# Projections with the weights moving: 512 or 416 columns a bank in place of 256

## The chip, the cores and the metric

The kernel runs on one core of a Trainium2 chip. The metric is the device time of one execution in microseconds (us). A core has a matrix engine (TensorE, PE in the rows), a vector engine (VectorE, DVE), a scalar engine (ScalarE, ACT), a general engine (GpSimd, POOL) and an engine that issues the transfers here (SyncE, SP). They run side by side and wait for each other through semaphores.

## The reference, cut to what matters

Two layers over x of 512 tokens and 1024 features, and a memory of 256 tokens. The first layer mixes with A (attention over all tokens) and B (a window with a sink), the second with C (attention through low-rank latents) and D (a neighbourhood of the token grid). Each layer goes on with a cross-attention into the memory and a gated feed-forward part. The projections that the change touches are these:

```python
def mixer_ab(h, w_in, g_qa, g_ka, sink, w_out, ang_1d, ang_2d):
    qa, ka, va, qb, kb, vb = _split(h @ w_in, AB_SIZES)        # 512, 128, 128, 512, 128, 128
    qa = apply_rope(rms_norm(qa.reshape(B, S, A_HEADS, HEAD_DIM), g_qa), ang_2d)
    ...
    qb = apply_rope(qb.reshape(B, S, B_HEADS, HEAD_DIM), ang_1d)
    ...

def mixer_cd(h, w_in, g_cq, g_ckv, w_uq, w_ukv, rpb, w_out, ang_c):
    cq, ckv, kr, qd, kd, vd = _split(h @ w_in, CD_SIZES)       # 256, 128, 32, 512, 512, 512
    q = (rms_norm(cq, g_cq) @ w_uq).reshape(B, S, C_HEADS, C_NOPE + C_ROPE)
    ...

def memory_cross_attention(h, m, w_q, w_kv, w_o):
    k, v = jnp.split(m @ w_kv, 2, axis=-1)                     # 512, 512
    ...
```

## The kernel before, in words

Every product is made in three matmuls. `split` (L111) takes a matrix apart into a rounded high part and the low part that is left; `mm3` (L126 to 129) adds high x high (L127), high x low (L128) and low x high (L129) into one bank. The high part of weights is a cast on ACT (L117), or on POOL (L119) where an engine is named; the low part a subtraction (L123) on DVE, for some weights on POOL. x is held transposed, with features on the partitions: `xh` and `xl` are eight tiles each, one for every 128 features.

Weights come through three rings of buffers: `load` (L98) brings 1 MB or less by one transfer of SP's queue into one of two `raw` buffers, `split` writes its parts into one of four `wh` and one of four `wl` buffers of 1024 columns. A raw buffer is free once both parts are made, a `wh` and `wl` once the last matmul has read them. A bank holds 512 columns; there are two banks `mm`, two `S`, two `T`, one `X` and one `O`.

In the projections of this change x stays in the array and the weights move through it, so the tokens come out on the partitions. `natural` (L194) does this for 256 columns of weights: a bank takes two token tiles of 128 beside each other, 24 matmuls each, and then `evac` reads the bank. `natural_weights` (L190) makes two parts of four k-rows (blocks of 128 features) for it.

Mixers A and B (`mixer_ab`, L369): `kv_part` makes keys and values, `q_part` (L461) the queries of four heads in one call, so that each mixer calls it twice. Its `evac` scales and rotates the heads of one token tile (`rotate`, L411, with ACT at L415, `headnorm` for A, `rope_mul` at L364 to 367 on POOL and DVE), writes high and low halves (L471, L472), and transposes them on PE (L429). Then 32 units of attention, each one head and half of the tokens, go through `pipeline` with lags: scores (L492, L493) into S, softmax (`softmax_rows`, L239), transposes of the weights into T (L272), a high and a low part of them (L275, L276), product with the values (L550).

Mixer C (`mixer_cd`, L555): the latents are two calls of `natural`, at column 256 for the keys' and values' latents with the shared rotary key (L619, 160 of its 256 columns are used) and at column 0 for the queries' (L620). `lat_norm` (L590) normalizes on ACT (L594, L595) and DVE (L598). On the way the row sums of x squared are brought over the partitions: eight matmuls (L150), a power on DVE and POOL (L133, L134), four scalings of the identity on DVE (L183), and one matmul that spreads them (L185). `latT` transposes the latents (L625). `up_pair` (L635) makes keys, values and queries of two heads from them: 256 columns of `w_ukv`, and of `w_uq` 256 columns of which 192 are used, for it is called four times. `v_d` (L565) makes the values of mixer D by `natural` into banks T.

`memory_kv` (L817) makes the memory's keys and values for the cross-attention, the values by two loads of 256 columns with the low parts turn by turn on DVE and POOL.

No order of the engines' work is written by hand: the program is written once, and a planner that simulates time puts each engine's instructions in an order when the kernel is built. Each engine then runs its own list strictly in that order.

## Time and profile before

| what | us |
|---|---|
| median of 3 runs | 1412.44 (1411.24 to 1412.59) |
| profiled execution | 1410.33 |
| its span in the trace | 1408.3 |
| PE busy | 1374.1, 98% |
| DVE busy | 796.6, 57% |
| ACT busy | 632.8, 45% |
| POOL busy | 413.1, 29% |
| mean granted clock of PE | 0.997 |

The span is the time from the first to the last instruction of the core; the execution is 2.0 us longer. A busy engine is one with an instruction open; for PE the rows of consecutive matmuls overlap, so a matmul costs the distance from its start to the next one's. A granted clock of 1.00 is the full 2.4 GHz, 0.50 the lower level of 1.2 GHz. In a row's end, `[2.82 <-DVE ptl L276]` says that the engine stood still for 2.82 us before it and that a DVE instruction of line 276 on the tile ptl released it. `mm<-wh,xgh` reads: into mm, from wh (moving) and xgh (in the array).

### The profile page before, as it was taken

How to read it: one execution, taken by the hardware profiler on the slowest of the kernel's cores; microseconds unless marked ns; L12 is line 12 of the kernel's file. 1: busy time of each engine (PE TensorE's matmuls, PEld its weight loads, DVE VectorE, ACT ScalarE, POOL GpSimd, SP SyncE). 2: the span in 40 equal slices, each digit the busy share in tenths (PEclk: the TensorE clock that was granted, in tenths of full speed). 3: DMA queues.
4: the chain of work that ended last, by engine and by line, in shares of the span. 5: the costliest groups of instructions: out<-in, count | busy, mean ns of one | idle time of the engine just before them, and what ended most of it. 6: DMA issues, size and time to landing. Idle time of an engine off the chain costs nothing.

```text
span 1408.3 us, 20396 instructions
## 1 busy us (share of the span) xinstructions
PE 1374.1 (98%) x7835; PEld 1194.8 (85%) x7835; DVE 796.6 (57%) x1426; ACT 632.8 (45%) x1217; POOL 413.1 (29%) x503
## 2 busy tenths in 40 slices
PE   8898999999999999999999999999999999999997
PEld 8897889998888888888988888798988888888887
DVE  6988886763344334436578744657643353335355
ACT  5567785643221323323468554656533222222243
POOL 4855444212210121111324345752122111111121
PEclk9999999999999999999999999999999999999999
DMA  7110024321332223203221132324302322232111
GB/s 235 61 61 30 23 70 132 122 106 60 100 110 90 90 94 114 85 23 105 51 76 46 31 101 66 113 97 149 121 30 92 114 93 90 90 106 104 45 45 61
DMA packets 77514, 120.88 MB, mean 86 GB/s; under 512 B 5791, under 2 KB 64106, under 8 KB 71786
## 3 DMA queue, kind: packets, MB, share of 16 engines
q1 hardware_dynamic: 77418, 119.58, 26.3%
q8 instruction: 62, 1.02, 0.3%
q14 instruction: 34, 0.28, 0.1%
HBM read 117.47 MB, written 2.10 MB: 85 GB/s over the span
## 4 chain that ended last, share of the span: by engine, by line
PE 87%; DVE 8%; ACT 2%; issue 1%; DMA 1%; POOL 0%; SPq 0%; POOLq 0%; ACTq 0%; DVEq 0%
PE mm L127 12%; PE mm L128 12%; PE mm L129 12%; PE S L127 7%; PE S L128 7%; PE S L129 7%; PE T L128 6%; PE T L129 6%; PE T L127 6%; PE O L550 3%; PE T L272 2%; DVE wl L123 1%; PE X L129 1%; PE O L129 1%; PE X L127 1%
## 5 line engine op out<-in xcount | busy, mean ns | idle before, releaser
L117 ACT CAST wh<-rawgu 128x1024 fp32r<-128x1024 f32 x88 | 92.3, 1053 | 296.4 <-PE S L128 116.4
L117 ACT CAST wh<-raw 128x1024 fp32r<-128x1024 f32 (+2 forms) x116 | 115.0, 992 | 198.8 <-PE mm L128 53.4
L1029 POOL TENSOR_TENSOR act<-P,act 128x512 fp32r<-128x512 f32 x44 | 74.2, 1688 | 401.0 <-ACT act L1028 401.0
L127 PE MATMUL T<-xgh,wh 128*128 128x512 f32 x352 | 137.8, 391 | 0.0
L123 DVE TENSOR_TENSOR wl<-raw,wh 128x1024 fp32r<-128x1024 f32 (+2 forms) x98 | 123.3, 1260 | 24.8 <-ACT wh L117 23.5
L128 PE MATMUL S<-xgl,wh 128*128 128x512 f32 x352 | 137.2, 390 | 0.0
L127 PE MATMUL S<-xgh,wh 128*128 128x512 f32 x352 | 136.9, 390 | 0.1
L129 PE MATMUL S<-xgh,wl 128*128 128x512 f32 x352 | 137.0, 389 | 0.0
L129 PE MATMUL T<-xgh,wl 128*128 128x512 f32 x352 | 137.0, 389 | 0.0
L128 PE MATMUL T<-xgl,wh 128*128 128x512 f32 x352 | 136.9, 389 | 0.0
L123 DVE TENSOR_TENSOR wl<-rawgu,wh 128x1024 fp32r<-128x1024 f32 x88 | 116.4, 1325 | 28.5 <-ACT wh L117 27.9
L1025 DVE TENSOR_TENSOR P<-P,T 128x512 f32<-128x512 f32 x44 | 30.1, 688 | 138.5 <-PE T L129 137.1
L253 POOL TENSOR_SCALAR P<-P,sm 128x512 f32<-128x512 f32 (+2 forms) x128 | 81.5, 650 | 83.2 <-DVE sm L251 48.3
L1022 DVE TENSOR_TENSOR g<-S,bc 128x512 f32<-128x512 f32 x44 | 30.2, 691 | 130.5 <-PE S L129 124.9
L128 PE MATMUL mm<-act,wh 128*128 128x512 f32 (+1 forms) x264 | 99.0, 375 | 0.0
L127 PE MATMUL mm<-act,wh 128*128 128x512 f32 (+1 forms) x264 | 98.9, 375 | 0.0
L129 PE MATMUL mm<-act,wl 128*128 128x512 f32 (+1 forms) x264 | 98.8, 375 | 0.0
L276 DVE TENSOR_TENSOR ptl<-T,pth 128x512 fp32r<-128x512 f32 (+2 forms) x128 | 72.4, 583 | 21.1 <-ACT pth L275 20.7
L127 PEld LDWEIGHTS S<-xgh,wh 128*128 128x128 f32 x352 | 66.1, 188 | 14.7 <-DVE g L1022 0.9
L127 PEld LDWEIGHTS T<-xgh,wh 128*128 128x128 f32 x352 | 66.1, 188 | 14.2 <-issue 0.5
L128 PEld LDWEIGHTS T<-xgl,wh 128*128 128x128 f32 x352 | 66.1, 188 | 14.1 <-issue 0.5
L129 PEld LDWEIGHTS S<-xgh,wl 128*128 128x128 f32 x352 | 66.1, 188 | 13.7
(366 smaller groups left out, 3811.9 us busy)
## 6 DMA issues: line engine op xcount, KB each, us to landing
rawgu<-in_w_gate_up_dram SPq DMA_DIRECT2D x44, 1024.0 KB, 5.0
raw<-in_w_down_dram SPq DMA_DIRECT2D x16, 1024.0 KB, 5.2
raw<-in_w_xkv_dram SPq DMA_DIRECT2D x8, 1024.0 KB, 5.2
raw<-in_w_down_dram SPq DMA_DIRECT2D x8, 768.0 KB, 4.7
raw<-in_w_in_ab_dram SPq DMA_DIRECT2D x5, 1024.0 KB, 5.5
raw<-in_w_out_ab_dram SPq DMA_DIRECT2D x4, 1024.0 KB, 5.1
raw<-in_w_xq_dram SPq DMA_DIRECT2D x4, 1024.0 KB, 5.3
raw<-in_w_xo_dram SPq DMA_DIRECT2D x4, 1024.0 KB, 5.2
```

The lines of the kernel that those rows point to most:

```text
L117: nc.scalar.copy(hv, v)
L123: low.tensor_sub(lv[:, q], v[:, q], hv[:, q].bitcast(F32))
L127: nc.tensor.matmul(o, lh, rh, start=start, stop=False)
L128: nc.tensor.matmul(o, lh, rl, start=False, stop=False)
L129: nc.tensor.matmul(o, ll, rh, start=False, stop=stop)
L253: nc.gpsimd.tensor_scalar(p, p, ri[:, j:j + 1], 1.0, op0=ALU.mult, op1=ALU.mult)
L272: nc.tensor.transpose(tb_[:, i * P:(i + 1) * P], p[:, i * P:(i + 1) * P], ident)
L276: nc.vector.tensor_sub(ptl[:, k0:k1, j * P:(j + 1) * P], tv, hv.bitcast(F32))
L550: nc.tensor.matmul(ob[:, q0 + a:q0 + b], v_of(kt), pt[:, kt, a:b], start=(i == 0 and j == 0), stop=(i == n - 1 and j == 1), skip_group_che ...
L1022: nc.vector.tensor_mul(g, bg, bc)
L1025: nc.vector.tensor_mul(sg, sg, bu)
L1029: nc.gpsimd.tensor_sub(l, sg, h.bitcast(F32))
```

## The change

Two functions are new. `wide_weights` loads eight k-rows of n columns in two transfers of four k-rows and splits each in two, so that one projection's weights stand in four pairs of buffers of two k-rows. `wide` puts one token tile into a bank, n columns wide, and calls `evac` for every tile.

- The queries of A and of B are one projection of 512 columns each. The rotation runs over eight heads at a time; the high parts of all of A's query weights are made on POOL, before only those of the first call.
- The latents of C are one projection of 416 columns (queries' 0 to 255, keys' and values' 256 to 383, rotary key 384 to 415) in place of two of 256.
- `w_uq` is taken by 192 columns a pair, not 256.
- The memory's values are one projection of 512 columns; all their low parts are made on DVE.

```diff
+    def wide_weights(w, c0, n, eng=None):
+        parts = []
+        for i in range(2):
+            v = load(w[4 * i * P:4 * (i + 1) * P, c0:c0 + n].rearrange("(k p) n -> p k n", p=P), 4, n)
+            parts += [split(v[:, 2 * j:2 * j + 2], 2, n, eng) for j in range(2)]
+        return parts
+
+    def wide(xh, xl, parts, n, evac, nt=NT):
+        for tt in range(nt):
+            bank = mm_bank()[:, :n]
+            ts_ = slice(tt * P, (tt + 1) * P)
+            for k in range(KF):
+                wh, wl = parts[k // 2]
+                mm3(bank, xh[k][:, ts_], xl[k][:, ts_], wh[:, k % 2], wl[:, k % 2], k == 0, k == KF - 1)
+            evac(tt, bank)
...
-            def rotate(src3, scale, cs, tt, nh, norm):
-                rt = ph.tile([P, 3, 256], F32, tag="rt", bufs=4, name="rt")
+            def rotate(rt, src3, scale, cs, tt, nh, norm):
...
+            def rt_tile():
+                return ph.tile([P, 3, S], F32, tag="rt", bufs=2, name="rt")
...
             def q_part(isA, c0):
-                Q = [ph.tile([P, 2, S], F32R, tag="Q", bufs=4, name="Q") for _ in range(2)]
-                def evac(b, bank):
-                    n = ph.tile([P, 2, 4, P], F32R, tag="nst", bufs=2, name="nst")
-                    for j in range(2):
-                        tt = 2 * b + j
-                        qs = bank[j].rearrange("p (h d) -> p h d", h=4)
-                        r = rotate(qs, (rstd if isA else rstd8)[:, tt:tt + 1],
-                                   tabs["q"] if isA else tabs["B"], tt, 4, isA)
-                        alternate("qs").tensor_copy(n[:, j, :, 0:64], r)
-                        nc.vector.tensor_sub(n[:, j, :, 64:128], r, n[:, j, :, 0:64].bitcast(F32))
-                    to_stacks(n, Q, b)
-                natural(xh, xl, w_in, c0, evac, natural_weights(w_in, c0, nc.gpsimd) if isA and c0 == 0 else None)
+                Q = [ph.tile([P, 4, S], F32R, tag="Q", bufs=2, name="Q") for _ in range(2)]
+                def evac(tt, bank):
+                    n = ph.tile([P, 8, P], F32R, tag="nst", bufs=2, name="nst")
+                    r = rotate(rt_tile(), bank.rearrange("p (h d) -> p h d", h=8), (rstd if isA else rstd8)[:, tt:tt + 1],
+                               tabs["q"] if isA else tabs["B"], tt, 8, isA)
+                    alternate("qs").tensor_copy(n[:, :, 0:64], r)
+                    nc.vector.tensor_sub(n[:, :, 64:128], r, n[:, :, 0:64].bitcast(F32))
+                    for i in range(2):
+                        t = x_bank()
+                        for a in range(4):
+                            nc.tensor.transpose(t[:, a * P:(a + 1) * P].bitcast(F32R), n[:, 4 * i + a], identr)
+                        nc.scalar.copy(Q[i][:, :, tt * P:(tt + 1) * P], t.rearrange("p (a n) -> p a n", a=4))
+                wide(xh, xl, wide_weights(w_in, c0, S, nc.gpsimd if isA else None), S, evac)
                 return Q
...
-                    sa["Q"] += q_part(True, 0) + q_part(True, 256)
+                    sa["Q"] += q_part(True, 0)
...
-                    sb_["Q"] += q_part(False, 768) + q_part(False, 1024)
+                    sb_["Q"] += q_part(False, 768)
...
-            natural(xh, xl, w_in, 256, ckv_evac)
-            natural(xh, xl, w_in, 0, cq_evac)
+            def evac(tt, bank):
+                lat_norm(bank[:, 256:384], ckn[:, tt], tt, 128)
+                rw = ph.tile([P, 3, 32], F32, tag="rw", bufs=2, name="rw")
+                nc.scalar.activation(rw[:, 0], bank[:, 384:416], AF.Copy, scale=rstd[:, tt:tt + 1])
+                rope32(krn[:, tt:tt + 1], rw[:, 0:1], rw[:, 1:2], rw[:, 2:3],
+                       tcs[0][:, tt:tt + 1], tcs[1][:, tt:tt + 1])
+                lat_norm(bank[:, 0:256], cqn[tt // 2][:, tt % 2], tt, 256)
+            wide(xh, xl, wide_weights(w_in, 0, 416), 416, evac)
...
-                c0 = min(pr * 192, 512)
-                off = pr * 192 - c0
-                v = load(w_uq[0][:, c0:c0 + 256].rearrange("(k p) n -> p k n", p=P), 2, 256)
-                wh, wl = split(v, 2, 256)
+                v = load(w_uq[0][:, pr * 192:(pr + 1) * 192].rearrange("(k p) n -> p k n", p=P), 2, 192)
+                wh, wl = split(v, 2, 192)
...
-        for c in range(2):
-            v = load(wkv[:, 512 + c * 256:512 + (c + 1) * 256].rearrange("(k p) n -> p k n", p=P), KF, 256)
-            pr = [split(v[:, 4 * i:4 * i + 4], 4, 256, None, alternate("kv")) for i in range(2)]
...
+        def v_evac(t, bank):
+            parts(bank.rearrange("p (h d) -> p h d", h=2), vm)
+        wide(mh, ml, wide_weights(wkv, 512, S), S, v_evac, 2)
...
-                    mm3(ob, vm[0][c][:, k, vs], vm[1][c][:, k, vs], pth[:, k], ptl[:, k], k == 0, k == 1)
+                    mm3(ob, vm[0][k][:, c, vs], vm[1][k][:, c, vs], pth[:, k], ptl[:, k], k == 0, k == 1)
```

Lines behind the new functions have higher numbers in the changed kernel: L594 is L617 there, L595 is L618, L615 is L632, L625 is L642. In all PE issues 6851 rows of order where it issued 7233.

Two places of the engines' orders. The first is PE's list at the start of mixer C, around the row sums of the normalization. Before (34 matmuls of the same three kinds stand between L150 and L185):

```order
L128 MATMUL mm<-wl,xgh 128x256
L129 MATMUL mm<-wh,xgl 128x256
L150 MATMUL X<-ones,P 128x1 x4
L127 MATMUL mm<-wh,xgh 128x256
...
L129 MATMUL mm<-wh,xgl 128x256
L185 MATMUL X<-P,ones 128x512
```

and with the change:

```order
L129 MATMUL mm<-wh,xgl 128x416
L127 MATMUL mm<-wh,xgh 128x416
L150 MATMUL X<-ones,P 128x1 x4
L128 MATMUL mm<-wl,xgh 128x416
L129 MATMUL mm<-wh,xgl 128x416
L185 MATMUL X<-P,ones 128x512
L127 MATMUL mm<-wh,xgh 128x416
```

L185 stands two matmuls behind the sums, where it stood 34 behind them. 46 matmuls of the latents stand ahead of L150 in the change, and 48 behind L185.

The second is ACT's list over the latents, with the first cast of weights behind them: the up-projection's, 256 columns of `w_ukv`, then those of `w_uq`, then v_d's of 1024. Before:

```order
L594 ACTIVATE P<-mm,sm 128x128
L615 ACTIVATE rw<-mm,sm 128x32
L595 ACTIVATE P,sm<-P 128x128
L117 CAST wh<-raw 128x256
L595 ACTIVATE P,sm<-P 128x128
L594 ACTIVATE P<-mm,sm 128x128
```

and with the change:

```order
L617 ACTIVATE P<-mm,sm 128x128
L632 ACTIVATE rw<-mm,sm 128x32
L618 ACTIVATE P,sm<-P 128x128
L617 ACTIVATE P<-mm,sm 128x256
L117 CAST wh<-raw 128x256
L618 ACTIVATE P,sm<-P 128x256
L117 CAST wh<-raw 128x384
```

Before, the cast stood behind the first two token tiles of the first latents; now it stands behind the third of four tiles of the joined projection.

## Rows read from the trace of the kernel before

**Rows 1.** The page: busy time of TensorE, and shares of the chain.

```profile
PE 1374.1 (98%) x7835; PEld 1194.8 (85%) x7835; DVE 796.6 (57%) x1426; ACT 632.8 (45%) x1217; POOL 413.1 (29%) x503
...
PE 87%; DVE 8%; ACT 2%; issue 1%; DMA 1%; POOL 0%; SPq 0%; POOLq 0%; ACTq 0%; DVEq 0%
```

**Rows 2.** Windows: us, busy (x) of PE, PEld, DVE, ACT, POOL; clock; DMA; GB/s.

```profile
24.00:61.00 37.00, 35.17 (x295) 34.76 (x295) 35.72 (x92) 15.71 (x31) 31.32 (x41) 1.00 0.41 127
61.00:125.00 64.00, 60.11 (x463) 55.42 (x461) 57.30 (x117) 46.02 (x107) 38.71 (x55) 1.00 0.10 34
...
676.00:702.00 26.00, 25.13 (x202) 24.21 (x201) 11.96 (x39) 10.49 (x31) 9.24 (x15) 1.00 0.25 63
...
960.00:1010.00 50.00, 49.52 (x382) 47.66 (x382) 34.86 (x68) 30.15 (x69) 13.18 (x20) 1.00 0.39 131
```

**Rows 3.** Timeline of PE, 695.7 to 696.6: start, length, line, operation, shape.

```profile
695.76 0.28 PE L129 MATMUL mm<-wh,xgl 128*128 128x256 f32 x1
...
696.60 0.28 PE L127 MATMUL mm<-wh,xgh 128*128 128x256 f32 x1
```

**Rows 4.** Timeline of PE, 600.0 to 601.2.

```profile
600.06 0.39 PE L127 MATMUL S<-xgh,wh 128*128 128x512 f32 x1
...
601.19 0.39 PE L129 MATMUL S<-xgh,wl 128*128 128x512 f32 x1
```

**Rows 5.** Timeline of PE, 158.3 to 159.1.

```profile
158.49 0.28 PE L550 MATMUL O<-ptl,vst 128*128 128x128 f32 x1
158.60 0.67 PE L127 MATMUL mm<-o,wh 128*128 128x512 f32 x2
```

**Rows 6.** Groups by form, DVE, 20 to 170: busy us, mean ns, idle before.

```profile
L276 DVE TENSOR_TENSOR ptl<-T,pth 128x512 fp32r<-128x512 f32 x32 | 21.5, 683 | 3.4 <-ACT pth L275 3.2
...
L276 DVE TENSOR_TENSOR ptl<-T,pth 128x256 fp32r<-128x256 f32 x3 | 1.3, 417 | 0.0
```

**Rows 7.** Timeline of all engines, 122.6 to 129.

```profile
124.89 0.40 PE L493 MATMUL S<-K,Q 128*128 128x512 f32 x1
...
127.28 0.68 DVE L276 TENSOR_TENSOR ptl<-T,pth 128x512 fp32r<-128x512 f32 x1
...
128.11 0.63 PE L272 MATMUL T<-identr,P 128*128 128x128 f32 x4 [2.82 <-DVE ptl L276]
```

**Rows 8.** Windows of 2 us behind that place, columns as in rows 2.

```profile
130.00:132.00 2.00, 1.97 (x9) 1.70 (x9) 1.94 (x4) 1.78 (x6) 0.51 (x2) 0.50 0.80 274
132.00:134.00 2.00, 2.00 (x14) 1.96 (x13) 2.00 (x5) 1.37 (x3) 1.46 (x2) 0.67 0.00 0
```

**Rows 9.** Timeline, 676.2 to 690.3: the first latents and the row sums.

```profile
676.22 0.28 PE L127 MATMUL mm<-wh,xgh 128*128 128x256 f32 x1
...
687.31 0.37 ACT L594 ACTIVATE P<-mm,sm 128x128 f32<-128x128 f32 x1 [5.32 <-POOL sm L134]
687.31 0.87 DVE L183 TENSOR_SCALAR P<-identr,sm 128x128 f32<-128x128 f32 x4 [1.13 <-POOL sm L134]
...
690.00 0.59 PE L185 MATMUL X<-P,ones 128*128 128x512 f32 x1
```

**Rows 10.** Timeline, 688.5 to 702.7: the weights behind the latents.

```profile
688.76 0.41 ACT L117 CAST wh<-raw 128x256 fp32r<-128x256 f32 x1 [0.17 <-PE mm L129]
...
689.20 0.42 DVE L123 TENSOR_TENSOR wl<-raw,wh 128x256 fp32r<-128x256 f32 x1 [0.17 <-ACT wh L117]
...
689.65 0.37 SPq L101 DMA_DIRECT2D raw<-in_w_in_cd_dram  x1
...
701.12 1.05 ACT L117 CAST wh<-raw 128x1024 fp32r<-128x1024 f32 x1 [2.69 <-PE mm L129]
...
702.20 1.23 DVE L123 TENSOR_TENSOR wl<-raw,wh 128x1024 fp32r<-128x1024 f32 x1 [2.46 <-ACT wh L117]
...
702.36 0.60 PE L625 MATMUL X<-identr,P 128*128 128x128 f32 x4
```

**Rows 11.** DMA issues, 685 to 705: KB each, median us to landing.

```profile
raw<-in_w_in_cd_dram SPq DMA_DIRECT2D x1, 1024.0 KB, 5.8
```

More of the change, by code (lines that the diff above doesn't have):

```diff
@@ L439, in evac @@
                     n = ph.tile([P, 2, 4, P], F32R, tag="nst", bufs=2, name="nst")
+                    rt = rt_tile()
                     for j in range(2):
@@ L442, in evac @@
                         ks = bank[j][:, 0:128].rearrange("p (h d) -> p h d", h=2)
-                        r = rotate(ks, rstd[:, tt:tt + 1], tabs["k"] if isA else tabs["B"], tt, 2, isA)
+                        r = rotate(rt[:, :, j * 256:(j + 1) * 256], ks, rstd[:, tt:tt + 1], tabs["k"] if isA else tabs["B"], tt, 2, isA)
                         rb = r.unsqueeze(2).broadcast_to([P, 2, 2, 64])
@@ L483, in front @@
                         st["pre"](h)
-                    Q, K = st["Q"][h // 2], st["K"][kv]
+                    Q, K = st["Q"][h // 4], st["K"][kv]
                     tiles, offs = [], []
@@ L490, in front @@
                         sb = s_bank()[:, :n]
-                        qv = Q[:, h % 2, qt * P:(qt + 1) * P]
+                        qv = Q[:, h % 4, qt * P:(qt + 1) * P]
                         nc.tensor.matmul(sb, qv, K[:, 0, k0 * P:k1 * P], start=True, stop=False)
@@ L604, in rope32 @@
                 nc.vector.tensor_add(dst, t1, t2)
-            def cq_evac(b, bank):
-                for j in range(2):
-                    lat_norm(bank[j], cqn[b][:, j], 2 * b + j, 256)
-            def ckv_evac(b, bank):
-                for j in range(2):
-                    tt = 2 * b + j
-                    lat_norm(bank[j][:, 0:128], ckn[:, tt], tt, 128)
-                    rw = ph.tile([P, 3, 32], F32, tag="rw", bufs=2, name="rw")
-                    nc.scalar.activation(rw[:, 0], bank[j][:, 128:160], AF.Copy, scale=rstd[:, tt:tt + 1])
-                    rope32(krn[:, tt:tt + 1], rw[:, 0:1], rw[:, 1:2], rw[:, 2:3],
-                           tcs[0][:, tt:tt + 1], tcs[1][:, tt:tt + 1])
-            natural(xh, xl, w_in, 256, ckv_evac)
-            natural(xh, xl, w_in, 0, cq_evac)
+            def evac(tt, bank):
[6 more added lines that the diff above has]
+            wide(xh, xl, wide_weights(w_in, 0, 416), 416, evac)
             def latT(src_of, g):
@@ L665, in up_pair @@
                         for k in range(2):
-                            mm3(bank[:, j * 256:(j + 1) * 256], cqT[k][0][:, ts_], cqT[k][1][:, ts_],
+                            mm3(bank[:, j * 192:(j + 1) * 192], cqT[k][0][:, ts_], cqT[k][1][:, ts_],
                                 wh[:, k], wl[:, k], k == 0, k == 1)
@@ L669, in up_pair @@
                         tt = 2 * b + j
-                        bv = bank[:, j * 256 + off:j * 256 + off + 192].rearrange("p (h d) -> p h d", h=2)
+                        bv = bank[:, j * 192:(j + 1) * 192].rearrange("p (h d) -> p h d", h=2)
                         nc.scalar.copy(nat[:, tt, 0], bv)
@@ L862, in memory_kv @@
             parts(bank.rearrange("p (m n) -> p m n", m=2), kT)
-        for c in range(2):
-            v = load(wkv[:, 512 + c * 256:512 + (c + 1) * 256].rearrange("(k p) n -> p k n", p=P), KF, 256)
-            pr = [split(v[:, 4 * i:4 * i + 4], 4, 256, None, alternate("kv")) for i in range(2)]
-            bank = mm_bank()
-            for t in range(2):
-                for k in range(KF):
-                    wh, wl = pr[k // 4]
-                    mm3(bank[:, t * 256:(t + 1) * 256], mh[k][:, t * P:(t + 1) * P],
-                        ml[k][:, t * P:(t + 1) * P], wh[:, k % 4], wl[:, k % 4], k == 0, k == KF - 1)
-            parts(bank.rearrange("p (t n) -> p t n", t=2), vm)
+        def v_evac(t, bank):
+            parts(bank.rearrange("p (h d) -> p h d", h=2), vm)
+        wide(mh, ml, wide_weights(wkv, 512, S), S, v_evac, 2)
         return kT, vm
```

## The prediction

> **What bounds the kernel now.** I read the page first, then the windows by stage, then the timeline of the places that the change touches. TensorE is busy 1374.1 us of a span of 1408.3, and 87% of the chain that ended last is matmuls [rows 1]. So a us saved on PE can be a us of time, but only in a stretch where nothing else ends last. The windows [rows 2] tell the stretches apart: around the memory's values of the second layer (960 to 1010) PE is busy 49.52 of 50; at the start of mixer C/D (676 to 702) 25.13 of 26; in mixers A/B it is 35.17 of 37 with DVE at 35.72, then 60.11 of 64 with DVE at 57.30. There PE and DVE are nearly level, and a saving on one alone may become a wait for the other.
>
> **What a matmul costs by its width.** PE's rows follow each other, so the price is the distance between starts, not the length shown. With 256 columns seven steps take 0.84 us, 0.120 each [rows 3]; with 512 five steps take 1.13, 0.226 each [rows 4]. One matmul of 512 in place of two of 256 saves 0.240 - 0.226 = 0.014 us. The line through both gives 0.120 + 160 x 0.106 / 256 = 0.186 us for 416 columns. Narrow ones stop gaining: 128 columns before a matmul with fresh weights still take 0.11 us [rows 5], so 192 columns are put at 0.11 (the line gives 0.093; the weights set the floor). The Trainium skill gives less for the pairs: its page "TensorE: Matmul & The Clock Gate", section "Back-to-back issue gap", has an isolated gap of N/2.4 plus 2.5 ns at full clock, so a pair joined would save only 2.5 ns and the 288 pairs of queries and values 0.7 us. By the rows here it is 14 ns and 4.1 us, and they decide.
>
> **The sum on PE.** Queries of A and B: 192 pairs x 0.014 = 2.7 us. Memory's values: 48 pairs a layer, 0.7 us each. Latents: 192 matmuls of 256 become 96 of 416, 96 x (0.240 - 0.186) = 5.2 us. Up-projection of C's queries: 96 matmuls x 0.01 = 1.0 us. Together 10.3 us, the ceiling of what narrower or longer streams alone can give.
>
> **Mixers A/B (with the first layer's values).** Of 3.4 us on PE I take 2.4. The rotation of the queries runs once a token tile with twice the columns: some 40 DVE instructions fewer. Two sizes of one instruction [rows 6] put the fixed part at 2 x 417 - 683 = 151 ns, at most 6 us; but the low parts of the values, now always on DVE and not on POOL every other time, bring two of 1.23 us [rows 10] back. So DVE is a little relieved, not overloaded; I hold back 1.0 us for the first stretch, where both are level. Bounds: above, a wait like the one at 124.89. There PE ran dry for 2.82 us, because DVE did pieces of the rotation ahead of the low part that the transposed scores needed [rows 7], and then the granted clock was 0.50 and 0.67 for 2 us each [rows 8], which is 1.0 + 0.7 = 1.7 us more. The planner orders the wider pieces anew; a second such gap costs 4.5, less 0.5 of the saving: +4. Below: this gap goes too, -3.4 - 4.5 = -7.9.
>
> **Start of mixer C/D.** Here I part from the ceiling; this is the term that decides. Before, the first latents start at 676.22 and end at 702.36 [rows 9, 10]. Three waits change:
>
> 1. The row sums' broadcast (L185) needs DVE's four scalings, done at 687.31 + 0.87 = 688.2 [rows 9]. Before, 34 matmuls stood between the sums and L185, which came at 690.00 and waited for nothing. Now 46 matmuls x 0.186 end at 684.8, the sums take some 0.8, two matmuls follow, and L185 stands there at 686.0: it waits 2 us. Then the first bank must be read: ACT begins with it at 687.31 [rows 9], needs four pieces instead of two, and I put the bank's release at 688.9. The remaining 48 matmuls take 9.0 us: latents end at about 697.9, 4.5 earlier than before.
> 2. What follows is v_d, the neighbourhood mixer's values, and its weights are late. There are two raw buffers and four high/low buffers. The latents' weights now come in four parts of two k-rows and hold all four; before, the cast of the up-projection's first weights found a free one at 688.76, its low part came at 689.20, and the load of v_d's weights into the raw buffer so freed was issued at 689.65 [rows 10]. Now that cast must wait until the last token tile has read part 0, six matmuls into it: 697.9 - (24 - 6) x 0.186 = 694.5. Add 0.41 and 0.42 for cast and low part and the issue: the load starts at 696.3. It took 5.8 us here [rows 11], so it lands at 702.1.
> 3. The cast (1.05) ends at 703.1, the low part (1.23) at 704.4. Before, that low part began at 702.20 and ended at 703.4 [rows 10]. So v_d's second matmul, which needs it, comes 0.9 us later than before, though PE was done 4.5 us earlier. PE stands still from 698.3 to 703.1.
>
> That idle stretch is longer than the one after which the clock fell [rows 7, 8], so 0 to 1.7 us more may go; I take the middle, 0.8. Net: 0.9 + 0.8 = +1.7. Bounds: -7 if the load were early (5.2 and the two waits for late x columns, which slower k steps hide), +2.6 with the whole clock loss.
>
> **The rest.** Up-projections beyond the first pair lie among C's attention units, where PE is not always last: 0.3 of the 1.0 (bounds 0 and 1.0). Second layer's values: all 0.7, in a stretch with PE at 99% [rows 2]; no DVE piece there is near the end. Bounds 0 and 0.7. Everything else (the wider buffers of Q, one-tile evacuation, the other index of the values in cross-attention) issues the same work: 0.
>
> **Sum:** -2.4 + 1.7 - 0.3 - 0.7 = -1.7 against the profiled execution's 1410.33: 1408.6. The median of the runs, 1412.44, is 2.1 above that execution, so on the median 1410.7.
>
> **Rivals.**
> - *All of it arrives.* If the planner gets the up-projection's cast ahead, or v_d's wait hides work that waited anyway, PE's 10.3 us come: 1402.1. For it: PE is 98% busy [rows 1]. Against: the four buffers are all held, and the cast stands behind the last tiles in ACT's order. Chance 0.22.
> - *Slower by a dry PE.* v_d's late weights cost 2.6 us with the clock at half, and the wider rotation makes one more gap in A/B (+4) or the saving there is lost (0): 1412.44 - 1.0 + 2.6 + (0 to 4) = 1414 to 1418, middle 1416. It decides at the landing of v_d's weights: later than the end of the latents, it has begun; PE idle there for over 5 us, it wins. For it: rows 7 and 8 show price and place of such a gap. Against: one gap alone is paid for by the savings elsewhere. Chance 0.17. The Trainium skill says the same of such waits (same page, "HAM oscillation — how this bites in real kernels": PE that waits for a DMA between bursts of matmuls is put back to the lower clock); the trace agrees as far as [rows 8] go, 0.50 behind a wait, though for DVE, not a DMA.
> - *The change does not do what it says.* 192 columns run no faster than 256, and 416 cost nearly 512's price: 96 x 0.014 = 1.3 in place of 5.2 and the 1.0 gone. Rows 5 speak against it in part. With the C/D wait shorter by what the latents take longer, the time is near -1: 1411.5. Chance 0.11.
> - My forecast, 0.5: 1410.7, its own range 1407 to 1414.
>
> **How the numbers follow.** A measurement of this kernel can tell about 0.2%, 2.8 us. Faster means below 1409.6: all of the first rival (0.22) and a third of the forecast (0.16): 0.38. Slower means above 1415.3: most of the second rival (0.13), a little of the others (0.03): 0.16. Same: 0.46. The range leaves out the best tail of the first rival and the upper part of the second: 1403.5 to 1416.5.
>
> **What would show it.** Right: latents' matmuls 0.186 apart; L185 waiting about 2 us for DVE; the cast of the up-projection's weights near 694 to 695, v_d's load behind it, and a PE wait of 4 to 5 us before v_d, with the granted clock below 1 in the window behind it; A/B shorter by about 2 us. Wrong: v_d's load issued before 691 (then the first rival), no clock loss behind the wait, latents at 0.21 or more, or an A/B stretch that ends later than before.

## The result and the profile after

The changed kernel takes 1432.49 us (median of 4 runs, 1425.74 to 1435.27), the kernel before 1411.84 in the runs beside it (4 runs, 1410.64 to 1412.59): ratio 1.014 [1.010, 1.018]. It is 20.7 us slower, and 16 us above the end of the range.

The profiled execution takes 1435.27 us, 24.9 more than the one before; its span is 1433.5 at a mean granted clock of 0.984, before 1408.3 at 0.997. The page, its row on busy time, as [rows 1]:

```profile
PE 1381.2 (96%) x7451; PEld 1183.2 (83%) x7451; DVE 795.9 (56%) x1386; ACT 627.6 (44%) x1207; POOL 402.7 (28%) x465
```

PE issues fewer matmuls and is busy 7 us longer: part of it runs at the lower clock. Span times (1 - clock) says how much time the lower clock accounts for if all of the span scaled with it: 22.9 us here, 4.2 before, so **up to 18.7 of the 24.9 us**. It is an upper figure: a low clock while PE stands still costs nothing. The windows, columns as in [rows 2], show where; the third and fourth lie in the second:

```profile
24.00:61.00 37.00, 32.14 (x170) 27.49 (x170) 32.62 (x66) 11.76 (x21) 27.43 (x29) 0.95 0.41 127
61.00:125.00 64.00, 57.14 (x321) 48.34 (x321) 48.71 (x88) 37.32 (x81) 35.56 (x39) 0.90 0.16 50
...
70.00:78.00 8.00, 6.34 (x20) 5.03 (x21) 7.98 (x20) 5.31 (x14) 4.95 (x7) 0.57 0.33 100
118.00:125.00 7.00, 4.19 (x17) 3.55 (x17) 5.13 (x10) 5.76 (x16) 2.50 (x3) 0.57 0.37 127
...
212.00:252.00 40.00, 37.69 (x215) 32.42 (x214) 26.35 (x52) 22.84 (x46) 13.37 (x18) 0.92 0.33 106
...
702.00:726.00 24.00, 18.32 (x92) 16.87 (x92) 8.63 (x30) 10.82 (x32) 5.89 (x15) 0.79 0.20 58
726.00:760.00 34.00, 31.96 (x232) 29.11 (x231) 23.70 (x66) 21.85 (x64) 7.29 (x16) 0.95 0.26 67
```

Length times (1 - clock) gives 1.9 + 6.4 + 3.2 + 5.0 + 1.7 = 18.2 us; the 6.4 are two places, 3.4 from 70 to 78 and 3.0 from 118 on. What PE waited for, by line (us in total, times, longest), has an entry for each of these places (the last window is the tail of the one ahead of it); before, the gap of [rows 7] was one such:

```profile
PE T L127 <- ACT wh L117: 5.4, 1, 5.4
PE mm L127 <- ACT rt L432: 4.6, 2, 4.0
...
PE S L515 <- ACT P L263: 3.3, 2, 2.8
...
PE X L495 <- ACT Q L496: 2.5, 2, 1.6
...
PE mm L127 <- DVE o L311: 2.1, 2, 1.9
...
PE X L185 <- DVE P L183: 1.9, 1, 1.9
```

In order of time these are the queries of A (53.6 and 70.8), attention of A and B (120.9), the product behind B (244.8), the row sums (701.8) and v_d (719.3): six places. The first instructions of some stages say where the lead of the kernel before grew. The first layer's gate projection begins 13.6 us later (318.95, before 305.33; in the six other kernels below whose edit leaves the first layer alone it begins at 305.5 to 307.7, so up to 2.4 of the 13.6 need not be the change's). C's first scores begin 18.7 us later (744.20, before 725.50), the second layer's gate projection 25.3 (1046.63, before 1021.38). The last 6.6 us grow where the granted clock is 1.00: from 760 to 860 PE is busy 95.1 of 100 us, before 98.1.

**Mixer A** (timeline of all engines: start, length, engine, line):

```profile
50.94 1.21 DVE L123 TENSOR_TENSOR wl<-raw,wh 128x1024 fp32r<-128x1024 f32 x1
...
52.07 0.68 DVE L491 TENSOR_TENSOR nst<-rt,nst 128x512 fp32r<-128x512 f32 x1
...
52.67 3.19 DVE L123 TENSOR_TENSOR wl<-raw,wh 128x1024 fp32r<-128x1024 f32 x2
...
52.84 0.69 ACT L432 ACTIVATE rt<-mm,sm 128x512 f32<-128x512 f32 x1 [2.63 <-DVE nst L491]
...
53.59 0.38 PE L127 MATMUL mm<-wh,xgh 128*128 128x256 f32 x1 [4.04 <-ACT rt L432]
```

PE wants a bank `mm`. ACT frees it by reading it into a rotation tile `rt`; the ring now has two of them, and one is free when DVE has subtracted the low half (L491) of an earlier token tile. DVE's list has a weight's low part of 1.21 us ahead of that, and two more, 3.19 together, behind. The place was tight before: there the same wait is 1.8 us (what PE waited for, 40 to 80, of the kernel before).

```profile
PE mm L127 <- ACT rt L415: 1.8, 1, 1.8
```

At 70.8 PE waits again, 1.60 us, for the copy of A's transposed queries (L496), and the clock is 0.57 from 70 to 78.

**Attention of A and B** (timeline, same columns; the first row is from before, the last from the second layer of the change):

```profile
98.16 0.37 SPq L820 DMA_DIRECT2D mn<-in_mem_dram  x1
...
111.81 0.37 SPq L835 DMA_DIRECT2D mn<-in_mem_dram  x1
...
116.99 0.63 ACT L839 ACTIVATE junk<-mn 128x512 f32<-128x512 f32 x1 [3.40 <-DMA mn<-in_mem_dram]
...
120.06 0.69 ACT L263 ACTIVATE P<-S,sm 128x512 f32<-128x512 f32 x1
...
120.90 0.80 PE L515 MATMUL S<-K,Q 128*128 128x512 f32 x1 [2.81 <-ACT P L263]
...
882.23 0.63 ACT L839 ACTIVATE junk<-mn 128x512 f32<-128x512 f32 x1 [2.25 <-DMA mn<-in_mem_dram]
```

The load of the memory for the cross-attention (`mn`) is issued at 111.81, before at 98.16. ACT's list has the squares of the memory (L839) at the place that the planner thought right: ACT stands 3.40 us, the exponentials (L263) behind it come late, and PE waits for the bank S. In the second layer ACT stands 2.25 us for the same load, before 0.27. No part of the change touches this load.

**Start of C and D** (timeline; the last row is from the DMA issues, 700 to 725):

```profile
701.79 1.23 PE L185 MATMUL X<-P,ones 128*128 128x512 f32 x2 [1.87 <-DVE P L183]
...
703.16 0.55 PE L128 MATMUL mm<-wl,xgh 128*128 128x416 f32 x1
...
705.94 0.41 PE L127 MATMUL mm<-wh,xgh 128*128 128x416 f32 x1
...
707.70 0.35 PE L127 MATMUL mm<-wh,xgh 128*128 128x416 f32 x1
...
709.03 0.35 PE L128 MATMUL mm<-wl,xgh 128*128 128x416 f32 x1
...
711.06 0.37 SPq L101 DMA_DIRECT2D raw<-in_w_in_cd_dram  x1
...
713.37 0.49 PE L642 MATMUL X<-identr,P 128*128 128x128 f32 x3
...
718.19 1.99 ACT L117 CAST wh<-raw 128x1024 fp32r<-128x1024 f32 x2 [3.03 <-DMA raw<-in_w_in_cd_dram]
...
719.29 0.80 PE L127 MATMUL T<-wh,xgh 128*128 128x256 f32 x2 [5.43 <-ACT wh L117]
```

```profile
raw<-in_w_in_cd_dram SPq DMA_DIRECT2D x1, 1024.0 KB, 7.1
```

Less the 13.6 us that the first layer lost, the latents end at 699.7 (before 702.4), v_d's weights are asked for at 697.4, and v_d starts at 705.7. Seven steps of 416 columns take 1.33 us, 0.190 each; behind the 1.87 us wait eight take 2.78, 0.348 each.

### The profile page after: what moved, and what is told of

It reads as the page before. It is cut to its first block, busy times and chain, and to the rows that moved or that the text cites. A ratio compares the mean times of both kernels' runs of the same rounds, so it can differ in the third digit from the quotient of the medians.

```text
span 1433.5 us, 19529 instructions
## 1 busy us (share of the span) xinstructions
PE 1381.2 (96%) x7451; PEld 1183.2 (83%) x7451; DVE 795.9 (56%) x1386; ACT 627.6 (44%) x1207; POOL 402.7 (28%) x465
## 3 DMA queue, kind: packets, MB, share of 16 engines
q1 hardware_dynamic: 72298, 118.93, 25.3%
## 4 chain that ended last, share of the span: by engine, by line
PE 83%; DVE 7%; ACT 3%; DMA 2%; POOL 2%; issue 2%; SPq 0%; POOLq 0%; ACTq 0%; DVEq 0%
PE mm L127 11%; PE mm L128 11%; PE mm L129 11%; PE S L127 7%; PE S L128 7%; PE S L129 7%; PE T L128 6%; PE T L129 6%; PE T L127 6%; PE O L573 3%; PE T L290 2%; DVE wl L123 1%; DVE ptl L294 1%; PE X L129 1%; PE O L129 1%
## 5 line engine op out<-in xcount | busy, mean ns | idle before, releaser
L117 ACT CAST wh<-raw 128x1024 fp32r<-128x1024 f32 (+3 forms) x114 | 111.7, 981 | 206.4 <-PE mm L128 70.1
L123 DVE TENSOR_TENSOR wl<-raw,wh 128x1024 fp32r<-128x1024 f32 (+3 forms) x102 | 132.1, 1296 | 31.5 <-ACT wh L117 30.1
```

What stands on the lines that cost most here:

```text
L117: nc.scalar.copy(hv, v)
L123: low.tensor_sub(lv[:, q], v[:, q], hv[:, q].bitcast(F32))
```

## The experiments

Each kernel is laid out anew by the planner, so a difference holds the edit and the order that came with it. "Clock" below is the mean over a kernel's runs of span times (1 - granted clock), less the same of the runs of before beside it; the clock is listed to 0.001, which is 1.4 us a run. "Rest" is what is left of the difference of the mean times.

| kernel | median us | ratio to before [95%] | difference | clock | rest |
|---|---|---|---|---|---|
| q_only | 1418.5 | 1.0052 [1.0032, 1.0072] | +7.0 | +2.8 | +4.2 |
| lat_only | 1419.6 | 1.0050 [1.0030, 1.0070] | +7.4 | +5.0 | +2.4 |
| uq_only | 1415.5 | 1.0029 [1.0016, 1.0043] | +3.9 | +3.8 | 0.0 |
| v_only | 1411.9 | 1.0002 [0.9993, 1.0011] | +0.3 | -0.2 | +0.4 |
| q_a | 1416.3 | 1.0032 [1.0020, 1.0045] | +4.5 | +2.2 | +2.3 |
| q_a_half | 1413.5 | 1.0014 [1.0005, 1.0024] | +2.1 | +0.8 | +1.4 |
| q_b | 1409.9 | 0.9989 [0.9980, 0.9998] | -1.6 | -1.3 | -0.2 |
| uq_stream | 1414.2 | 1.0016 [1.0007, 1.0026] | +2.3 | +1.6 | +0.6 |
| uq_mem | 1410.0 | 0.9990 [0.9980, 1.0000] | -1.5 | +0.3 | -1.9 |
| after_mem | 1424.4 | 1.0093 [1.0078, 1.0108] | +12.9 | +9.1 | +3.8 |
| lat_own | 1414.2 | 1.0013 [1.0004, 1.0023] | +2.1 | +3.3 | -1.3 |
| lat_fill | 1412.7 | 1.0015 [1.0006, 1.0025] | +2.1 | +0.9 | +1.1 |
| ri_only | 1411.2 | 0.9995 [0.9986, 1.0004] | -0.6 | -0.7 | +0.1 |
| b_uq_ri | 1407.4 | 0.9969 [0.9957, 0.9981] | -4.5 | -2.3 | -2.2 |
| all_but_a | 1415.2 | 1.0026 [1.0016, 1.0035] | +3.4 | +2.8 | +0.6 |
| all_repaired | 1424.5 | 1.0081 [1.0054, 1.0108] | +12.2 | +7.4 | +4.9 |
| own2_all_but_a | 1413.4 | 1.0014 [1.0002, 1.0025] | +1.8 | +3.5 | -1.7 |
| own2_no_v | 1406.0 | 0.9963 [0.9952, 0.9974] | -5.1 | +0.4 | -5.5 |

### Each part alone

q_only, lat_only, uq_only and v_only are the kernel before with the lines of the diff for one part:

```diff
+                wide(xh, xl, wide_weights(w_in, c0, S, nc.gpsimd if isA else None), S, evac)   # q_only
+            wide(xh, xl, wide_weights(w_in, 0, 416), 416, evac)                               # lat_only
+                v = load(w_uq[0][:, pr * 192:(pr + 1) * 192].rearrange("(k p) n -> p k n", p=P), 2, 192)   # uq_only
+        wide(mh, ml, wide_weights(wkv, 512, S), S, v_evac, 2)                                 # v_only
```

> Only the queries of A and B take 512 columns; latents, up-projection and the memory's values stay as before. Theory one (the loss belongs to parts of the change; the queries' part is the wait of TensorE for the two score-wide banks, which the scalar engine reads only when a rotation tile is free): slower by 10 to 14 us, nearly all of it before the cross-attention, with the clock gaps near 50, 72 and 118 us of the trace. Rival (each part alone is cheap, the loss comes from their sum in shared buffer rings): within 3 us of before. My forecast's own step (saving 2.4 us) would be 1409 to 1410.

> Only the latents are one projection of 416 columns. Theory one (v_d's weights are late because the four buffers are held): v_d's first matmul about 3 us later than before, a TensorE wait of some 5.6 us ahead of it and a lower clock behind it; total slower by 4 to 11 us, all of it after the start of mixer C. Rival (the attention units' loss of 6 us comes from the narrower up-projection): slower by 3 to 5 us only.

> Only the up-projection of C's queries takes 192 columns. Theory one (the loss lies with the latents): within 2 us of before, 0 to 1 us faster. Rival (the narrower up-projection disturbs the attention units): slower by 3 to 6 us, between the first scores of C and the memory's keys.

> Only the memory's values take 512 columns a bank. Theory one: 0 to 1.4 us faster, both layers' value projections 0.7 us shorter. Rival (the low parts, now all on the vector engine, delay the last softmaxes of B): slower by 1 to 6 us, in the stretch around the memory's keys and values of the first layer, with B's last product with the values later.

q_only lies between its two expectations, lat_only in the first one's range, uq_only in the rival's. 0.52 + 0.50 + 0.29 + 0.02 = 1.33%, the whole 1.4%. That the sum fits is chance, for by stages the profiled executions do not add up. From the latents' start to C's first scores the parts add 0.1, 0.7, -0.3 and 0.0 us to the 49.28 of before, the change 5.1. From there to the second layer's gate projection they add 0.7, 8.4, 3.7 and 0.7 to 295.88, the change 6.6: lat_only and uq_only lose there to the same load (below), and the change loses it once. None of the four gains, though each saves PE's time.

### The queries: A against B

```diff
-                    sb_["Q"] += q_part(False, 768) + q_part(False, 1024)
+                    sb_["Q"] += q_narrow(False, 768) + q_narrow(False, 1024)   # q_a: B in two calls of 256 columns, in the joined buffers; q_b: the same for A
...
+                    for i in range(2):   # q_a_half: A's rotation over four heads, rt [P, 3, 256] with four buffers, as before
+                        r = rotate(rt_tile(), bank[:, i * 256:(i + 1) * 256].rearrange("p (h d) -> p h d", h=4), (rstd if isA else rstd8)[:, tt:tt + 1],
```

> A's queries take 512 columns, B's stay at two projections of 256 (with buffers of the joined size). The two theories split the loss of 6.8 us of the queries' part. Theory one (the joined projection holds all four weight buffers, so what is loaded next comes late: B's holding delays the output projection's weights and behind them the memory's load, for which the scalar engine stands still at 113 us): A alone keeps the wait near 49 us (4 us, one clock step of 1.7), and loses the wait near 118 us; slower than before by 1 to 4 us. Rival (the rotation over eight heads with two rotation tiles is too coarse, for A as for B): A, with its normalization the longer rotation, has most of it, slower by 4 to 7 us.

> B's queries take 512 columns, A's stay at two projections of 256. Theory one: the memory's load is issued at 108 us or later (98 before), the scalar engine waits for it with the casts and exponentials of the scores behind it, TensorE stands still for some 2.5 us near 118 us with the clock at half behind it; slower than before by 3 to 6 us, and no wait over 2.5 us near 49 us. Rival: under 2 us slower, the memory's load as early as before.

> As q_a (A's queries 512 columns wide, B's narrow), but the rotation runs over four heads at a time in four tiles of the old size, so the matmuls and the held weight buffers are as in q_a and the rotation is as before the change. Theory one (the rotation over eight heads is too coarse: the bank's release waits for a whole tile's chain): TensorE's wait near 48 us falls from 4.2 to below 2.5 and the 1.8 and 1.0 us waits near 70 us fall; 1410 to 1413. Rival (the weights' casts and low parts of four parts, ahead of the rotation in the queues of the vector and scalar engines, are what delays it): the waits stay and the time stays at 1415 to 1418.

The loss is A's: q_a is 4.5 us slower, q_b 1.6 faster, nearly all of that clock and not columns: the gap of [rows 7] is gone in its trace, and one of 3.77 us at 52.73 has come. Waits of PE, 40 to 80, first of q_a, then of q_a_half:

```profile
PE mm L127 <- ACT rt L432: 4.0, 1, 4.0
```

```profile
PE mm L127 <- ACT rt L432: 2.9, 1, 2.9
```

With the rotation and its four buffers as before, about half of A's loss goes (+2.1 left) and the wait shrinks by 1.1 us, but it stays; the lower clock behind 70, 0.50 and 0.73 in q_a from 72 to 76, is 1.00 there. So the wider rotation is half of A's term; the rest sits in the order of the weights' parts in ACT's and DVE's lists, which I did not isolate. In q_b the load `mn` is issued later still, at 118.16, but ACT waits 0.4 us for it, since its instruction stands later too. The chain that I expected there (late load, so long wait) failed: the place of the waiting instruction in the queue decides, not the load's time alone.

### The memory's load

```diff
-                            mm3(bank[:, j * 256:(j + 1) * 256], cqT[k][0][:, ts_], cqT[k][1][:, ts_],
-                                wh[:, k], wl[:, k], k == 0, k == 1)
+                            mm3(bank[:, j * 256 + off:j * 256 + off + 192], cqT[k][0][:, ts_], cqT[k][1][:, ts_],
+                                wh[:, k, off:off + 192], wl[:, k, off:off + 192], k == 0, k == 1)   # uq_stream
...
-            nc.scalar.activation(junk, mn[:, i // 2, i % 2 * S:(i % 2 + 1) * S], AF.Square, accum_out=ss[:, i:i + 1])
+            nc.scalar.activation(junk, still, AF.Square, accum_out=ss[:, i:i + 1])   # uq_mem, after_mem: still is xh[0]
```

> Only the matmuls of the up-projection of C's queries are narrower: 192 of the 256 columns, which are loaded and split as before. Theory one (the loss of uq_only comes from the new order, not from the price of a narrower matmul): 1410 to 1412.5, no lowered clock in mixers C and D; the pitch of these matmuls 0.10 to 0.115 us. Rival (a matmul of 192 columns is no cheaper or dearer, since its weights take longer to come): pitch 0.12 or more and slower by 1 us or more.

> As uq_only, but the sums of squares of the memory read a tile that is already there instead of the memory tile, so that the scalar engine does not wait for that load; the memory is normalized with the sums of another tile. Theory one (in uq_only the scalar engine stands 2.0 us at 858 us for the memory's load with the exponentials of the scores behind it, and TensorE thins out and drops to half clock at 867): no lowered clock between 850 and 880 us, 1410 to 1413, 2 to 4 us faster than uq_only. Rival (the lowered clock there comes from the new mixture of short matmuls): the clock falls there all the same and the time stays at 1414 to 1417.

> The whole change, with the sums of squares of the memory read from a tile that is already there, in both layers (the memory is normalized with the sums of another tile). Theory one: the scalar engine's waits of 3.4 us at 113 and 2.3 us at 880 go, with the clock step near 119; 4 to 9 us faster than the change, 1424 to 1429. Rival (other waits take their place, since the queries of B come late anyway): within 3 us of the change's 1432.

uq_stream loads and splits what the kernel before does; only matmuls are narrower, and it is 2.3 us slower. So that much of uq_only's loss is not in its smaller loads: the planner, told that some matmuls are shorter, wrote another order, and in it ACT stands 1.98 us for the second layer's memory (857.91), where before it stood 0.27. Its time is above the expected 1412.5. In uq_only ACT's row that waits for the memory, and the windows of 2 us behind it:

```profile
859.95 0.63 ACT L822 ACTIVATE junk<-mn 128x512 f32<-128x512 f32 x1 [2.01 <-DMA mn<-in_mem_dram]
```

```profile
864.00:866.00 2.00, 1.46 (x10) 0.90 (x8) 2.00 (x4) 1.95 (x5) 2.00 (x4) 1.00 0.00 0
866.00:868.00 2.00, 1.67 (x7) 0.99 (x6) 2.00 (x6) 1.14 (x4) 2.00 (x3) 0.67 0.34 98
868.00:870.00 2.00, 2.00 (x5) 1.61 (x6) 1.20 (x4) 0.00 (x0) 2.00 (x4) 0.50 0.03 5
```

PE is busy 1.46 of 2 us at 864, with no single wait over 0.5, and then the clock is 0.67 and 0.50. In uq_mem, whose squares read a tile that is long there, the same stretch:

```profile
864.00:868.00 4.00, 4.00 (x21) 3.03 (x20) 3.02 (x10) 1.84 (x6) 3.39 (x6) 1.00 0.37 101
868.00:872.00 4.00, 4.00 (x21) 3.36 (x19) 2.15 (x7) 1.93 (x5) 2.77 (x6) 1.00 0.62 215
```

uq_mem is 5.5 us below uq_only by medians (5.4 by means), after_mem 8.1 below the change (6.9). That is the price of an instruction that waits at the head of ACT's list for data that it has no hurry for, with the order that the planner wrote around it; the two were not told apart.

Four traces have such a wait of about 2 us in the second layer: the change (2.25), uq_only (2.01), uq_stream (1.98) and lat_only (1.96). From C's first scores to the second layer's gate projection these four take 299.4 to 304.2 us. Before takes 295.9, uq_mem 294.5, after_mem 294.9, and the other kernels at most 297.8, but for all_repaired with 299.8. So of what after_mem gives back, 2.6 us come ahead of the first layer's gate projection, by the profiled executions, and 7.6 in the second layer. How it is lost differs: in the change the clock is 1.00 and PE is busy less, in lat_only the clock is near 0.50 from 914 to 924, 50 us behind ACT's wait (864.09), so that there only this comparison speaks for the load.

### The latents

```diff
-    def split(v, a, b, eng=None, low=nc.vector):
+    def split(v, a, b, eng=None, low=nc.vector, own=None):   # lat_own: two of the four parts not in the rings wh, wl
...
+            parts += [split(v[:, 2 * j:2 * j + 2], 2, n, eng, own=own[j] if i == 0 else None) for j in range(2)]
...
+            own = [ph.tile([P, 4, S], F32R, tag="qk", bufs=2, name="own") for _ in range(2)]
```

```diff
+            idle = s_bank()   # lat_fill: lat_only and 30 transposes that nobody reads, ahead of v_d
+            for i in range(30):
+                nc.tensor.transpose(idle[:, i % 4 * P:(i % 4 + 1) * P], ckn[:, 2], ident)
```

> As lat_only, but two of the four weight parts of the latents lie in buffers of their own (those that C's attention units use later), so that the up-projection's weights find free buffers and v_d's load is issued early. Theory one (late weights by held buffers): v_d's load issued before 692 on the scale of the kernel before, TensorE's wait ahead of v_d 0 to 1.5 us in place of 3.9, no lowered clock right behind it, C's first scores 2 to 4 us earlier than in lat_only; total 1413 to 1417. Rival (the loss is the planner's new order in the attention units, whatever the load): C's first scores earlier, but the total as in lat_only, 1418 to 1421.

> As lat_only, with 30 more transposes into an unused bank in the 4 us in which TensorE waits for v_d's weights; they compute nothing. The matmuls behind them start no earlier. Theory one (the idle stretch lowers the clock): the lowered clock from 705.9 to 709.3 us goes and C's first scores come 1.5 to 2 us earlier after v_d's start than in lat_only. Rival (the clock falls for another reason there, and the filler only delays): the clock falls all the same, C's first scores come no earlier.

lat_only has the wait that was forecast, for v_d's cast, and a clock of 0.65 and 0.78 in the two windows of 3 us behind it:

```profile
704.47 0.50 PE L127 MATMUL T<-wh,xgh 128*128 128x256 f32 x2 [3.77 <-ACT wh L117]
```

```profile
705.00:708.00 3.00, 2.35 (x12) 2.27 (x12) 2.58 (x4) 2.43 (x4) 0.00 (x0) 0.65 0.02 5
708.00:711.00 3.00, 3.00 (x23) 3.00 (x23) 0.25 (x1) 0.00 (x0) 0.00 (x0) 0.78 0.33 87
```

lat_fill gives PE work for most of that wait, and the clock stays at 1.00:

```profile
699.76 3.44 PE L646 MATMUL S<-identr,P 128*128 128x128 f32 x30
...
705.09 0.50 PE L127 MATMUL T<-wh,xgh 128*128 128x256 f32 x2 [1.79 <-ACT wh L117]
```

```profile
705.00:708.00 3.00, 2.26 (x16) 2.03 (x17) 2.62 (x3) 2.97 (x5) 0.00 (x0) 1.00 0.00 0
708.00:711.00 3.00, 3.00 (x28) 3.00 (x27) 0.75 (x1) 0.08 (x1) 0.00 (x0) 1.00 0.31 87
```

From v_d's first matmul to C's first scores lat_only takes 23.80 us, lat_fill 21.46, before 22.79: the step behind the wait costs 2.3. From the latents' start the gain is only 1.0 (50.02, with the filler 48.97), since v_d's load took 6.7 us in lat_fill's execution and 5.4 in lat_only's. lat_fill is 6.9 us below lat_only in all by medians (5.3 by means); what goes beyond comes later, where its order has no wait for `mn`, so it does not speak for the filler. And lat_only's loss is mostly not where I looked for it: v_d starts 0.3 us earlier than before, measured from the latents' start, not 3 later; up to C's first scores 0.7 us are lost, and 8.4 from there to the second layer's gate projection. In lat_own v_d's load is issued at 681.19 and v_d waits for nothing; it is 5.4 us below lat_only, and its order has no wait for `mn` either. But C's first scores come no earlier: the borrowed buffers are free only when the feed-forward part ends, PE waits there for their cast (4.8 us in its list of waits), and the clock falls there instead. My expectation was right on v_d and wrong on where the gain would show.

### Putting it together

```diff
+    mem_ri = const.tile([P, 4], F32, name="mem_ri")   # ri: the memory's row factors are the same in both layers
...
+        ri = mem_ri
+        if layer == 0:
...
+            parts += [split(v[:, 2 * j:2 * j + 2], 2, n, eng, own=own[j] if i == 1 else None) for j in range(2)]   # own2
```

ri_only is before with ri; b_uq_ri is q_b, uq_only and ri; all_but_a adds the latents with lat_own's buffers and the memory's values; all_repaired is the whole change with ri, lat_own's buffers and A's rotation over four heads. The own2 kernels give the borrowed buffers to the last two parts, which are needed later, in all_but_a; own2_no_v leaves the memory's values as before.

> The kernel before, with the memory's row factors kept from the first layer for the second (they are the same), so that the scalar engine sums no squares of the memory in the second layer. A base for the next three. Both theories: within 1.5 us of before, since in the kernel before that wait was 0.3 us long.

> B's queries 512 wide, A's narrow, the up-projection 192 wide, row factors of the memory kept from the first layer. Theory one (the gains on TensorE are there once no load is late in an in-order queue): 1.5 to 4 us faster than before, 1407.5 to 1410. Rival (each new order has its own waits, so gains do not add): 1410 to 1414.

> All parts of the change but A's queries, with the two repairs: two weight parts of the latents in buffers of their own, the memory's row factors kept. Theory one: of the change's 20.7 us of loss nearly all is gone, 1407 to 1413. Rival (the planner's order, whatever the loads): 1416 to 1424.

> The whole change, with both repairs and with A's rotation over four heads at a time. Theory one: A's remaining 2 us and the memory's load of the first layer (still late behind the held weight buffers) stay, the rest goes: 1411 to 1419. Rival: 1422 or more.

> As own2_no_v, with the memory's values 512 wide too. Theory one (with the values ahead of B's last scores, TensorE has nothing left to do beside B's end, stands 2.0 us near 232 and 242 us and drops to half clock behind it, as in all_but_a and in the change): 2 to 6 us slower than own2_no_v. Rival (the values save TensorE 1.4 us): 0 to 1.5 us faster than own2_no_v.

> B's queries, the latents and the up-projection as in the change, A's queries and the memory's values as before; row factors of the memory kept; of the latents' weight parts the last two lie in buffers of their own, not the first two (in all_but_a the first two could be cast only when the feed-forward's buffers were free, and TensorE stood 3.6 us ahead of the latents). Theory one (causes found, gains on TensorE real): no wait over 1 us ahead of the latents and of v_d, no lowered clock between 670 and 730 us, 4 to 9 us faster than before: 1403 to 1408. Rival (joined latents bring a wait of their own wherever the buffers lie): 1408 or more, no faster than b_uq_ri.

ri alone does nothing: before, ACT waits 0.3 us for `mn`, once; b_uq_ri is 4.5 us below before, half of it clock. all_but_a and all_repaired came out slower than I expected of the repairs; all_but_a carries lat_own's fault:

```profile
684.10 0.68 PE L131 MATMUL mm<-own,xgh 128*128 128x416 f32 x2 [3.56 <-ACT own L121]
```

In own2_no_v that wait is gone; from 670 to 730 PE's longest wait is the one for the row sums (L189 there), the next is 1.0, and v_d's load is issued early (timeline):

```profile
PE X L189 <- DVE P L187: 2.1, 1, 2.1
```

```profile
679.68 0.37 SPq L101 DMA_DIRECT2D raw<-in_w_in_cd_dram  x1
```

**own2_no_v is the best, 1406.0 us: 5.8 below before by medians, 26.5 below the change.** Its gain is all in the rest (-5.5). That fits PE's shorter work, 5.2 + 1.0 for the latents and the up-projection and 1.3 for B by the prediction's prices, but is not shown to be that. With the memory's values joined as well (own2_all_but_a) it is 7.5 us slower, more than expected, though that part alone costs nothing. In its profile B's last product is late and PE waits behind it, 225 to 262, where own2_no_v has no wait over 0.6:

```profile
PE mm L131 <- DVE o L315: 1.9, 1, 1.9
```

The clock is 0.58 from 234 to 238, as it falls at the same place in the change (212 to 252, 0.92). The two profiled executions are 4 us apart. By the first layer's gate projection that is 3.0; from the latents' start to C's first scores it is 2.9 more, and these may be luck: PE waits 2.05 us for the row sums in both, and behind it the clock falls in own2_all_but_a (second row) and not in own2_no_v (first row, windows of 4 us). Then it wins 2 back.

```profile
690.00:694.00 4.00, 4.00 (x22) 3.92 (x21) 1.58 (x7) 1.66 (x8) 1.89 (x4) 1.00 0.02 4
```

```profile
690.00:694.00 4.00, 1.95 (x4) 0.90 (x4) 2.05 (x13) 2.40 (x10) 2.49 (x5) 0.66 0.00 0
```

all_repaired is 9 us above all_but_a, so A's queries cost more in company than alone (q_a_half +2.1), and with every repair the whole change is still 12 us slower than before. Why is open: the causes found account for a part of the loss.

## Why the prediction was wrong

**Right.** The prices by width: 416 columns at 0.190 (predicted 0.186), 192 at 0.111 (0.11). L185 waits 1.87 us (2). The load of v_d's weights at 697.4 on the old scale in the change, 695.9 in lat_only (696.3). The wait before v_d of 5.43 (4.8), and a lowered clock behind it, which went when lat_fill shortened that wait, by one trace of each. The load's time is partly luck: the sum 694.5 + 0.41 + 0.42 is 695.3, and in [rows 10] the issue follows the low part by 0.03, so 696.3 has 0.9 too much.

**The step that failed with the largest piece that one repair gave back: "Everything else ... issues the same work: 0".** The work is the same, its order is not. The load of the memory's rows, which I did not look at, became waits of 3.40 and 2.25 us for ACT, one in each layer, and taking them away (after_mem) gave back 7 to 8 of the 20.7 us, most of it in the second layer. With it fails the term for the up-projection's queries, -0.3 with 0 as its worse bound: alone it costs 3.9, all of it clock, and without ACT's wait nothing (uq_mem -1.5). I had bounded it by the matmuls themselves and not by what a shifted order can do.

**Mixers A/B, -2.4 (bounds -7.9 and +4).** q_only is +7.0, above the upper bound: by size this term was the furthest off. I relieved DVE by counting instructions; the point was how long a tile is held. One rotation tile of eight heads, two in the ring, keeps a bank until DVE comes to it, and low parts of 1.2 us or more stand in DVE's list. That is half of A's loss (q_a_half); the other half I did not isolate. B's half is -1.6, near the forecast by luck: it is clock (-1.3), where I had forecast columns (rest -0.2).

**Start of C/D, +1.7 (bounds -7 and +2.6).** The mechanism was right. Alone the size was too: in lat_only the stretch from the latents' start to C's first scores is 0.7 us longer than before. In the change it is 5.1 longer, beyond the bound. There v_d starts 2.95 us later, measured from the start of the latents, where I had 0.4 for its first matmul (703.1 against 702.71) and 0.9 for the second. Two pieces were missing: the clock fell already behind the wait at L185 (eight steps at 0.348 in place of 0.190, 1.3 us, and the load behind them late by 1.1), and the load took 7.1 us where before it took 5.8 [rows 11]. Neither belongs to the wait as such: lat_only waits the same 1.87 us at L185, and the clock stays at 1.00 behind it (windows).

```profile
690.00:694.00 4.00, 3.80 (x18) 3.31 (x19) 2.33 (x15) 2.75 (x12) 2.65 (x6) 1.00 0.00 0
```

Its load took 5.4 us. I priced the lower clock once, at half of 1.7; in 702 to 760 it is 5.0 + 1.7, of which up to 1.4 fall on the time in which PE waits for v_d anyway.

**Second layer's values, -0.7.** Alone +0.3, within its interval nothing. From 960 to 1010 PE is as full as in [rows 2], so the cover was read rightly:

```profile
960.00:1010.00 50.00, 49.07 (x286) 42.30 (x285) 34.25 (x50) 28.84 (x48) 14.58 (x17) 1.00 0.42 141
```

But the same function also makes the first layer's values, and joined with B's queries its order brings a wait at the end of B (own2_all_but_a).

**The rivals.** The slower one had the mechanism, a dry PE and then the lower clock, and gave it one more place in A/B beside v_d; there were six in all. Its top, 1418, is still 14 us below the result. Its chance of 0.17 was too low: rows 7 and 8 already showed that a gap of 2.8 us costs 1.7 more, and the planner writes a new order in every stretch that the change touches.

## What to carry to other kernels

Where a planner orders the queues, a small edit costs what the new order costs: look in every engine's list for an instruction that waits for a load and has urgent work behind it, and take that wait away before joining matmuls. When a join makes a tile or a ring's buffers wider, ask how long each is held and who waits for the next one, not how many instructions it saves. Put the lower clock behind every new PE wait of about 2 us into the range, each time it occurs, as something that may come or not: behind the wait for the row sums it cost 1.3 us in the change and nothing in lat_only. And compare parts with the whole stage by stage: here the totals added up and the stages did not.

## What was not expected of the hardware

- The clock also fell without a long wait: in uq_only PE was busy 1.46 of 2 us from 864 and 1.67 from 866, with no wait over 0.5, and the clock was 0.67 from 866 and 0.50 from 868.
- The same wait has the lower clock behind it in one trace and not in another. In the change 1.87 us at L185 were followed by 2.8 us of matmuls at 0.348 in place of 0.190; in lat_only, lat_fill and after_mem the same 1.87 us left the clock at 1.00. With 2.05 us it fell in own2_all_but_a and stayed in own2_no_v.
- One load of 1 MB, v_d's weights, took 5.4 us in lat_only, 5.8 before, 6.7 in lat_fill, 7.1 in the change and 7.4 in after_mem.
- The spread of the runs grew with the lost clock. Before, the four runs lie within 2 us; the change's within 9.5, and its slowest ran at a clock of 0.984, its fastest at 0.990: 0.006 of 1430 us is 8.6 us.
- With 3.44 us of transposes that nobody reads in the wait for v_d, the clock stayed at 1.00 (lat_fill, one trace).
